# Stick-breaking attention: the causal triangle as a product on TensorE in place of GpSimd's selections

## The chip, the cores and the metric

The kernel runs on one core of a Trainium2 chip. Its time is device microseconds of one execution; a time of a kernel is the median of several executions. The core has five engines, each with a queue of its own that it works through in order: TensorE (PE in the profile, its weight loads PEld), VectorE (DVE), ScalarE (ACT), GpSimd (POOL) and SyncE (SP, which issues DMAs). An instruction waits on semaphores for what other engines have to finish first.

## The reference, cut to what matters

Two transformer blocks run one after the other on 1024 tokens of width 1024. The change lies in the second block's attention, which has 8 heads of 64:

```python
for qb in range(s_len // Q_BLOCK):            # blocks of 128 queries
    z = jnp.einsum('bqhd,bkhd->bhqk', qi, kj) * scale
    causal = s_pos < t_pos
    log_beta = jax.nn.log_sigmoid(z)
    log_rem = jnp.where(causal, jax.nn.log_sigmoid(-z), 0.0)
    suffix = lax.cumsum(log_rem, axis=3, reverse=True) - log_rem
    weights = jnp.where(causal, jnp.exp(log_beta + suffix), 0.0)
    o = jnp.einsum('bhqk,bkhd->bqhd', weights, vj)
```

A weight is the sigmoid of its own score times the product of the sigmoids of the negated scores of all keys between it and the query. Keys at or after the query have a weight of 0, and a factor of 1 in the products.

## The kernel before

All is in fp32. A dense product is made of three products in fp32r, high part by high part, low by high, high by low. The tokens stand in reverse order, so that the suffix of the reference is a running product from the left.

The stage around the change (`ple1_mix2`, from 1625 to 2148 us in the profile) consists of two generators: `dense_in2`, which makes the input projections, the gating, the short convolution and the output projection (`dense_out2`), and `stick_breaking`. `merge_in` takes pieces of the two in an order written out by hand, the string `B_MERGE` (0 for the dense work, 1 for the attention, h for a hook, a piece of work that had been put off). With it the order of the instructions in every engine's queue is fixed; the engines then run each as soon as its semaphores allow.

`stick_breaking` goes through four head pairs p. For each it stacks high and low parts of q and k (`stack`, L1006 to L1024; the low parts get to their place by DMAs from GpSimd's queue), and then goes through 8 query blocks i and the two heads a, 64 blocks in all. Block i has w = 1024 - 128 i columns of keys. Its first 128 columns hold the triangle, the others are all visible. A block consists of these steps:

- L1922: the scores z, two products for each 512 columns, into the PSUM tile ps_s.
- L1925 and L1926 (recorded on L520, in the helper `act`): ScalarE makes rem = sigmoid(-z) and beta = sigmoid(z), both read from PSUM and written to SBUF.
- L1928 and L1929: GpSimd's selections, 128x128 each. The first puts 1 into rem where the key isn't visible, the second 0 into beta.
- L1930: VectorE's scan, a running product along rem.
- L1931: VectorE multiplies beta by the scan, shifted by one column.

Two blocks later (`SB_LAG`) `transposes` turns the weights on TensorE (L1859) in two groups of up to four; ScalarE copies the first group out of PSUM (L1862), VectorE the second (L1864). `product` (L1877) then multiplies by v, and ScalarE copies the result (L1879).

The dense pieces between these are `strip` (L252, with outputs of 128x512) and `token_pair` (L279). Their results leave PSUM on VectorE (L1631 in the projections, L1327 in the output projection, where they are added to x) or in part on ScalarE. Their weights come by DMA, are rounded to a high part by ScalarE (L206), and GpSimd, at times VectorE, makes the low part (L208, 128x1024). GpSimd also has other wide products of 128x1024: the convolution's L1753 and L1758, the gating's L1727, and low parts of the output projection's inputs (y1L, y3L, yb0L, yb1L, yb2L on L701).

At the stage's start `norm_R2` ends with L510 on VectorE, and `dense_in2` loads the gating's constants and lets GpSimd select the lower triangle of one of them, wsT (L1624). Small tiles come from the pool `cst` and stay there; `self.U` gives a tile of 128x1024 from a pool of 41, and it is free again when its last name is gone. `self.masks` (L786) is used in the first block only.

Of the kernel before, what the change touches and what calls it, by code (L numbers as in the profile page):

```python
# [8 lines left out]
F32R = mybir.dt.float32r  # L9
I32 = mybir.dt.int32  # L10
U8 = mybir.dt.uint8
AF = mybir.ActivationFunctionType
ALU = mybir.AluOpType
# [4 lines left out]
P = 128  # L18
# [124 lines left out]
class Kern:  # L143
# [639 lines left out]

    def load_masks(self):
        nc = self.nc
        self.masks = self.cst.tile([P, 8, P], U8, name="masks")  # L786
        t = self.U("mask_f")
        nc.sync.dma_start(out=t, in_=self.aps["c_masks"])
        nc.gpsimd.tensor_copy(out=self.masks, in_=t.rearrange("p (a b) -> p a b", b=P))
# [41 lines left out]
    def block1_mix(self):  # L831
        tc, nc = self.tc, self.nc
        self.scr_hg = self.dram.tile([16, P, 1024], F32, name="scr_hg")
        self.scr_hv = self.dram.tile([4, P, 1024], F32, name="scr_hv")
        self.scr_oda = self.dram.tile([4, P, 1024], F32, name="scr_oda")
        with tc.tile_pool(name="psA", bufs=1, space=PSUM) as psA:
            self.ps_o = self.ps_t = lambda: psA.tile([P, 512], F32, tag="t", name="ps_t", bufs=2)
            self.ps_s = self.ps_n = lambda: psA.tile([P, 1024], F32, tag="s", name="ps_s", bufs=2)
            self.ones = self.cst.tile([P, P], F32, name="ones")
            nc.vector.memset(self.ones, 1.0)  # L840
            self.one_col = self.ones[:, 0:1]
            self.Rc = self.cst.tile([P, 8], F32, name="Rc")

            ps = self.ps_t()[:, 0:P]
            for i in range(16):
                nc.tensor.matmul(ps, self.ones, self.ones, start=True, stop=True)
            ps = None
            self.set_ln()
            st = dict(H=[], L=[])
            xt = []  # L850
            for m in range(KD):
                t = self.U(f"x{m}")
                nc.sync.dma_start(out=t, in_=self.aps["xT"][m])
                xt.append(t)
                if m < 3:
                    self._w_dma(self.upool if m == 2 else None)
            self.load_consts()
            self.raw_qk = {}
            self.first_slots = []
            self.oT = {}  # L860
            self.x = None
            if A_MERGE:
                self.merge_in(A_MERGE, self.dense_mix(st, xt), self.diff_attention(), self.hgrn())
            else:
                self.merge(self.dense_mix(st, xt), self.diff_attention(), self.hgrn())
        self.more_ps = None
        self.dbg("x_mix", self.x)

    def dense_mix(self, st, xt):
# [740 lines left out]
    def dense_in2(self):  # L1610
        nc = self.nc
# [6 lines left out]
        for j in range(2):  # L1618
            for a in range(2):
                nc.sync.dma_start(out=bb[64 * a:64 * a + 64, j], in_=self.aps["sgu_b"][2 * j + a].partition_broadcast(64))  # L1620
        wsT = sgu_c[:, 512:1024].rearrange("p (g t) -> p g t", g=4)
        nc.sync.dma_start(out=wsT, in_=self.aps["sgu_w"])

# [226 lines left out]
    def stick_breaking(self):  # L1850
        nc = self.nc

        def transposes(u, g0):
            gn = min(4, u["n"] - g0)
            if g0 == 0:
                u["T"] = self.U("WT")
            ps = self.ps_t()
            for j in range(gn):
                nc.tensor.transpose(ps[:, j * P:(j + 1) * P], u["W"][:, (g0 + j) * P:(g0 + j + 1) * P], self.ident)  # L1859
            dst = u["T"][:, g0 * P:(g0 + gn) * P]  # L1860
            if g0 == 0:
                nc.scalar.copy(out=dst, in_=ps[:, 0:gn * P])  # L1862
            else:
                nc.vector.tensor_copy(out=dst, in_=ps[:, 0:gn * P])  # L1864
            if g0 + gn == u["n"]:
                u["W"] = None
                turned.append(u)
            return 109 * gn

        def product():  # L1870
            two, turned[:] = turned[:2], turned[2:]
            p, i, n, yb = (two[0][k] for k in ("p", "i", "n", "y"))
            ps = self.ps_o()
            for j in range(n):
                for a in range(2):
                    h = 2 * p + a
                    nc.tensor.matmul(ps[64 * a:64 * a + 64, 0:P], self.vsb[i + j][:, h * 64:(h + 1) * 64], two[a]["T"][:, j * P:(j + 1) * P],  # L1877
                                     start=(j == 0), stop=(j == n - 1))
            nc.scalar.copy(out=yb[:, i * P:(i + 1) * P], in_=ps[:, 0:P])  # L1879
            if i == 7:  # L1880
                self.dbg(f"y_b{p}", [yb])
                if p == 3:
                    self.yT[p] = self.split(yb, f"yb{p}")
                else:
                    nc.sync.dma_start(out=self.scr_y[4 + p], in_=yb)
                self.done.add(f"yb{p}")
            return 268 * n

        def drain(left):
            while len(queue) > left or len(turned) > 1:  # L1890
                if len(turned) > 1:
                    yield product(), 0
                else:
                    u = queue.pop(0)
                    for g0 in range(0, u["n"], 4):
                        yield transposes(u, g0), LAT["sb_t"]

        queue, turned = [], []
        for p in range(4):
            while f"q{p}" not in self.done or f"k{p}" not in self.done:  # L1900
                yield WAIT
            A, B = [], []
            yield from self.stack(self.raw_qk.pop(f"q{p}"), 0.125, "stationary", A)
            yield from drain(2)
            yield from self.stack(self.raw_qk.pop(f"k{p}"), 1.0, "moving", B)
            yield from drain(0)
            yield 0, LAT["sb_head"]
            while "vsb0" not in self.done or "vsb1" not in self.done:
                yield WAIT
            yb = self.U("yb")  # L1910
            for i in range(8):
                n = 8 - i
                w = n * P
                for a in range(2):
                    pd = queue.pop(0) if len(queue) > SB_LAG else None
                    if pd is not None:
                        yield transposes(pd, 0), 0
                    z = self.ps_s()
                    for c0 in range(0, w, 512):
                        cn = min(512, w - c0)  # L1920
                        for part in range(2):
                            nc.tensor.matmul(z[:, c0:c0 + cn], A[a][:, i * P:(i + 1) * P], B[a][part][:, i * P + c0:i * P + c0 + cn],  # L1922
                                             start=(part == 0), stop=(part == 1))
                    beta, rem = self.U("beta"), self.U("rem")
                    self.act(AF.Sigmoid, out=rem[:, 0:w], in_=z[:, 0:w], scale=-1.0)  # L1925
                    self.act(AF.Sigmoid, out=beta[:, 0:w], in_=z[:, 0:w])  # L1926

                    nc.gpsimd.affine_select(out=rem[:, 0:P], in_=rem[:, 0:P], pattern=[[1, P]], compare_op=ALU.is_gt, fill=1.0, base=0, channel_multiplier=-1)  # L1928
                    nc.gpsimd.affine_select(out=beta[:, 0:P], in_=beta[:, 0:P], pattern=[[1, P]], compare_op=ALU.is_gt, fill=0.0, base=0, channel_multiplier=-1)  # L1929
                    nc.vector.tensor_tensor_scan(out=rem[:, 0:w], data0=rem[:, 0:w], data1=self.one_col.to_broadcast([P, w]), initial=1.0, op0=ALU.mult, op1=ALU.min)  # L1930
                    nc.vector.tensor_tensor(out=beta[:, 1:w], in0=beta[:, 1:w], in1=rem[:, 0:w - 1], op=ALU.mult)  # L1931
                    queue.append(dict(p=p, i=i, n=n, W=beta, y=yb))
                    beta = rem = None
                    yield 0.84 * w, 0
                    if len(turned) > 1:
                        yield product(), 0
                    if pd is not None and pd["n"] > 4:
                        yield transposes(pd, 4), 0
                    yield 0, LAT["sb"] + LAT["sb_w"] * w / 1024
        A = B = None  # L1940
        yield 0, LAT["sb"]
        yield from drain(0)
# [277 lines left out]
```

## Time and profile before

| | us |
|---|---|
| median of 3 runs (2973.49 to 2975.86) | 2975.2 |
| the profiled execution | 2975.06 |
| its span, from the first instruction to the last | 2973.3 |
| head pairs of the attention, in the profile | 1753 to 1850, 1850 to 1950, 1950 to 2050, 2050 to 2148 |
| busy: TensorE / VectorE / ScalarE / GpSimd | 2805.6 / 1800.7 / 1150.7 / 976.3 |

A row of the waits names the engine and the instruction that waited, then the one that released it. In the timeline the bracket behind an instruction is the idle time of its engine before it, with the one that released it. PE's rows have modelled ends, and one product's end lies over the next one's start; distances between starts are the better measure. "Granted clock" is the share of TensorE's full clock of 2.4 GHz, of which the chip grants all or half, averaged over a stretch.

### The profile page before, as it was taken

What the parts mean: (1) busy time and instruction counts of PE and PEld (TensorE: products, weight loads), DVE (VectorE), ACT (ScalarE), POOL (GpSimd) and SP (SyncE); (2) the same over time, 40 slices, a digit from 0 to 9 for tenths busy, and PEclk for the clock granted to TensorE, in tenths of its full rate; (3) what the DMA queues carried; (4) which work ended last, traced back from release to release, by engine and by line L of the source; (5) the groups of instructions that cost most, each with busy time, mean ns of one, the idle gap of its engine ahead of it and who ended that gap; (6) DMA issues with size and microseconds to landing.
All of it is one profiled execution on the core that took longest, in us unless ns stands there. A gap on an engine that the chain in (4) does not pass through costs nothing. (4 is left out here: it accounts for less than half of the span.)

```text
span 2973.3 us, 35223 instructions
## 1 busy us (share of the span) xinstructions
PE 2805.6 (94%) x13976; PEld 2320.8 (78%) x13976; DVE 1800.7 (61%) x2090; ACT 1150.7 (39%) x1684; POOL 976.3 (33%) x647
## 2 busy tenths in 40 slices
PE   8999999989899999999999999878899999999999
PEld 7878878877778888777877887656677787888877
DVE  6277676888788777733446465678686444333344
ACT  4245444564543333321234434454364334112131
POOL 2320214665213333221335153343413442223141
PEclk9999999989999999999999999889999999999999
DMA  3321223231312222531113122033133226322112
GB/s 127 83 54 46 79 71 129 102 124 50 107 50 92 85 82 82 200 119 57 57 50 106 43 71 57 29 113 107 36 120 114 105 101 234 127 78 100 39 54 85
DMA packets 73956, 265.23 MB, mean 89 GB/s; under 512 B 8768, under 2 KB 9536, under 8 KB 73792
## 3 DMA queue, kind: packets, MB, share of 16 engines
q1 hardware_dynamic: 49216, 174.90, 16.4%
q10 hardware_dynamic: 20736, 75.51, 7.7%
q0 software_dynamic: 3840, 12.59, 2.0%
q8 instruction: 110, 1.80, 0.3%
q14 instruction: 54, 0.44, 0.0%
HBM read 187.46 MB, written 61.87 MB: 84 GB/s over the span
## 5 line engine op out<-in xcount | busy, mean ns | idle before, releaser
L208 POOL TENSOR_TENSOR WL<-raw,WH 128x1024 fp32r<-128x1024 f32 x120 | 307.1, 2560 | 992.0 <-ACT WH L206 852.7
L1327 DVE TENSOR_TENSOR xr<-xr,psd 128x512 f32<-128x512 f32 x296 | 202.3, 686 | 393.4 <-PE psd L252 391.0
L206 ACT ACTIVATE WH<-raw 128x1024 fp32r<-128x1024 f32 x144 | 151.9, 1056 | 410.6 <-PE psd L252 276.2
L458 PE MATMUL ps_f<-xT,WH 128*128 128x512 f32 x816 | 269.5, 392 | 7.6 <-ACT u L2007 4.9
L458 PE MATMUL psd<-x,WH 128*128 128x512 f32 x800 | 260.8, 392 | 3.8 <-DVE fr L2004 2.6
L252 PE MATMUL psd<-xH,WH 128*128 128x512 f32 x568 | 234.3, 413 | 3.2 <-DVE cv L1652 1.6
L252 PE MATMUL psd<-xL,WH 128*128 128x512 f32 x568 | 224.8, 396 | 0.0
L252 PE MATMUL psd<-xH,WL 128*128 128x512 f32 x568 | 224.4, 395 | 0.0
L458 PEld LDWEIGHTS ps_f<-xT,WH 128*128 128x128 f32 x816 | 153.3, 188 | 45.5 <-ACT u L2007 9.5
L458 PEld LDWEIGHTS psd<-x,WH 128*128 128x128 f32 x800 | 150.8, 189 | 37.8 <-issue 3.9
L458 PE MATMUL ps_f<-xT,WL 128*128 128x512 f32 x408 | 159.1, 390 | 1.6 <-DVE WL L443 1.5
L458 PE MATMUL psd<-x,WL 128*128 128x512 f32 x400 | 156.2, 391 | 0.0
L279 PE MATMUL psd<-WH,xH 128*128 128x256 f32 x448 | 130.0, 290 | 11.2 <-DVE hgst L978 8.8
L1930 DVE TENSOR_TENSOR_SCAN rem<-rem,ones 128x1024 f32<-128x1024 f32 (+7 forms) x64 | 91.6, 1431 | 77.8 <-POOL rem L1928 77.6
L252 PEld LDWEIGHTS psd<-xH,WH 128*128 128x128 f32 x568 | 108.9, 192 | 26.8 <-issue 4.8
L279 PE MATMUL psd<-WL,xH 128*128 128x256 f32 x448 | 128.1, 286 | 1.3 <-POOL WL L208 1.3
L279 PE MATMUL psd<-WH,xL 128*128 128x256 f32 x448 | 127.9, 285 | 0.0
L252 PEld LDWEIGHTS psd<-xL,WH 128*128 128x128 f32 x568 | 108.4, 191 | 24.1
L252 PEld LDWEIGHTS psd<-xH,WL 128*128 128x128 f32 x568 | 108.8, 192 | 21.9 <-issue 1.7
L443 DVE TENSOR_TENSOR WL<-S,WH 128x512 fp32r<-128x512 f32 x136 | 99.3, 743 | 43.7 <-ACT WH L441 43.5
L1102 DVE TENSOR_REDUCE nm<-ps_s 128x1 f32<-128x1024 f32 x64 | 77.6, 1219 | 49.2 <-PE ps_s L1101 49.1
L417 POOL TENSOR_TENSOR S<-raw_b 128x512 f32<-128x512 f32 x30 | 43.9, 1463 | 192.7 <-DMA raw_b<-w_gate 78.8
(809 smaller groups left out, 7595.2 us busy)
## 6 DMA issues: line engine op xcount, KB each, us to landing
raw<-w_in ACTq DMA_DIRECT2D x54, 512.0 KB
scr_f<-fr SPq DMA_DIRECT2D x54, 512.0 KB
fl<-scr_f SPq DMA_DIRECT2D x54, 512.0 KB
raw<-w_ff ACTq DMA_DIRECT2D x32, 512.0 KB
raw<-w_down ACTq DMA_DIRECT2D x22, 512.0 KB
raw_a<-w_ff SPq DMA_DIRECT2D x18, 512.0 KB
scr_hg<-hgst SPq DMA_DIRECT2D x16, 512.0 KB
hg<-scr_hg SPq DMA_DIRECT2D x16, 512.0 KB
```

Source lines behind the costliest of these rows:

```text
L206: nc.scalar.activation(out=self.WH[:, s], in_=raw, func=AF.Copy)
L208: eng.tensor_tensor(out=self.WL[:, s], in0=raw, in1=self.WH[:, s].bitcast(F32), op=ALU.subtract)
L252: nc.tensor.matmul(ps, a, b[:, hs], start=(i == 0), stop=(i == n - 1))
L279: nc.tensor.matmul(ps, a[:, ts], b, start=(i == 0), stop=(i == 23))
L417: diff = lambda out, x, y, op=ALU.subtract: (nc.vector if q["nsum"] < q["head"] + 3 else nc.gpsimd).tensor_tensor(out=out, in0=x, in1=y, o ...
L443: eng.tensor_tensor(out=WL, in0=src, in1=WH.bitcast(F32), op=ALU.subtract)
L458: self.nc.tensor.matmul(ps, x[:, js], y, start=(fresh and j == 0 and e == 0), stop=(j == 3 and e == 2), skip_group_check=True)
L1102: nc.vector.tensor_reduce(out=nm[:, m:m + 1], in_=sc, axis=AX.X, op=ALU.max, negate=True)
L1327: self.nc.vector.tensor_tensor(out=self.x[m][:, hs], in0=self.x[m][:, hs], in1=ps, op=ALU.add)
L1930: nc.vector.tensor_tensor_scan(out=rem[:, 0:w], data0=rem[:, 0:w], data1=self.one_col.to_broadcast([P, w]), initial=1.0, op0=ALU.mult, op1 ...
```

## The change

A constant tile `never` of 128x128 holds -2^100 where the key isn't visible and 0 elsewhere; a second one holds the identity. They are made at the start of `dense_in2`: VectorE clears a tile, GpSimd selects in it once, and ScalarE writes it and the identity as fp32r into the place of `self.masks`, which is given up after the first block. In each of the 64 blocks TensorE adds the product of the identity with `never` to the first 128 columns of the scores, after the first of their two products. The sigmoids then come out as 1 and 0 there, and both selections by GpSimd are dropped. `B_MERGE` and all else stay.

```diff
--- before.py
+++ after.py
@@ -783,7 +783,7 @@
 
     def load_masks(self):
         nc = self.nc
-        self.masks = self.cst.tile([P, 8, P], U8, name="masks")
+        self.masks = self.cst.tile([P, 8, P], U8, tag="masks", name="masks")
         t = self.U("mask_f")
         nc.sync.dma_start(out=t, in_=self.aps["c_masks"])
         nc.gpsimd.tensor_copy(out=self.masks, in_=t.rearrange("p (a b) -> p a b", b=P))
@@ -864,6 +864,7 @@
             else:
                 self.merge(self.dense_mix(st, xt), self.diff_attention(), self.hgrn())
         self.more_ps = None
+        self.masks = None
         self.dbg("x_mix", self.x)
 
     def dense_mix(self, st, xt):
@@ -1618,6 +1619,16 @@
         for j in range(2):
             for a in range(2):
                 nc.sync.dma_start(out=bb[64 * a:64 * a + 64, j], in_=self.aps["sgu_b"][2 * j + a].partition_broadcast(64))
+
+
+        t = self.U("never_f")[:, 0:P]
+        nc.vector.memset(t, 0.0)
+        nc.gpsimd.affine_select(out=t, in_=t, pattern=[[1, P]], compare_op=ALU.is_gt, fill=-2.0 ** 100, base=0, channel_multiplier=-1)
+        c = self.cst.tile([P, 2 * P], F32R, tag="masks", name="never")
+        self.never, self.ident_r = c[:, 0:P], c[:, P:2 * P]
+        nc.scalar.activation(out=self.never, in_=t, func=AF.Copy)
+        nc.scalar.activation(out=self.ident_r, in_=self.ident, func=AF.Copy)
+        t = None
         wsT = sgu_c[:, 512:1024].rearrange("p (g t) -> p g t", g=4)
         nc.sync.dma_start(out=wsT, in_=self.aps["sgu_w"])
 
@@ -1920,13 +1931,12 @@
                         cn = min(512, w - c0)
                         for part in range(2):
                             nc.tensor.matmul(z[:, c0:c0 + cn], A[a][:, i * P:(i + 1) * P], B[a][part][:, i * P + c0:i * P + c0 + cn],
-                                             start=(part == 0), stop=(part == 1))
+                                             start=(part == 0), stop=(part == 1), skip_group_check=True)
+                            if c0 + part == 0:
+                                nc.tensor.matmul(z[:, 0:P], self.ident_r, self.never, start=False, stop=False, skip_group_check=True)
                     beta, rem = self.U("beta"), self.U("rem")
                     self.act(AF.Sigmoid, out=rem[:, 0:w], in_=z[:, 0:w], scale=-1.0)
                     self.act(AF.Sigmoid, out=beta[:, 0:w], in_=z[:, 0:w])
-
-                    nc.gpsimd.affine_select(out=rem[:, 0:P], in_=rem[:, 0:P], pattern=[[1, P]], compare_op=ALU.is_gt, fill=1.0, base=0, channel_multiplier=-1)
-                    nc.gpsimd.affine_select(out=beta[:, 0:P], in_=beta[:, 0:P], pattern=[[1, P]], compare_op=ALU.is_gt, fill=0.0, base=0, channel_multiplier=-1)
                     nc.vector.tensor_tensor_scan(out=rem[:, 0:w], data0=rem[:, 0:w], data1=self.one_col.to_broadcast([P, w]), initial=1.0, op0=ALU.mult, op1=ALU.min)
                     nc.vector.tensor_tensor(out=beta[:, 1:w], in0=beta[:, 1:w], in1=rem[:, 0:w - 1], op=ALU.mult)
                     queue.append(dict(p=p, i=i, n=n, W=beta, y=yb))
```


## Rows read from the trace of the kernel before

**Rows 1.** the page's first part: busy time, share of the span, instructions
```profile
PE 2805.6 (94%) x13976; PEld 2320.8 (78%) x13976; DVE 1800.7 (61%) x2090; ACT 1150.7 (39%) x1684; POOL 976.3 (33%) x647
```

**Rows 2.** stretch, its us, busy us (x count) of PE, PEld, DVE, ACT, POOL; clock; DMA
```profile
1753.00:1850.00 97.00, 93.75 (x577) 75.50 (x576) 66.38 (x71) 46.97 (x76) 40.22 (x44) 1.00 0.21 58
1850.00:1950.00 100.00, 86.62 (x469) 68.90 (x469) 64.92 (x68) 45.16 (x73) 38.02 (x38) 0.90 0.11 34
1950.00:2050.00 100.00, 79.61 (x439) 61.58 (x440) 77.11 (x84) 55.91 (x89) 40.54 (x45) 0.88 0.35 107
2050.00:2148.00 98.00, 79.92 (x462) 61.48 (x462) 68.46 (x71) 40.19 (x72) 42.07 (x46) 0.93 0.24 74
```

**Rows 3.** waits of PE, 1753 to 2148: us in total, times, longest
```profile
PE ps_t L1877 <- DVE WT L1864: 9.7, 7, 3.6
PE ps_t L1859 <- DVE WT L1864: 7.7, 3, 4.4
PE psd L252 <- DVE y0L L701: 7.5, 1, 7.5
PE psd L252 <- DVE xr L1327: 5.0, 2, 2.8
```

**Rows 4.** all waits, 1750 to 2150
```profile
POOL rem L1928 <- ACT rem L520: 161.2, 51, 16.9
DVE rem L1930 <- POOL rem L1928: 77.6, 41, 8.2
```

**Rows 5.** timeline, one block: start, us, engine, line, operation, [idle before <-releaser]
```profile
2089.26 0.92 ACT L520 ACTIVATE rem<-ps_s 128x896 f32<-128x896 f32 x1 [0.91 <-PE ps_s L1922]
2090.26 0.30 POOL L1928 TENSOR_SCALAR_AFFINE_SELECT rem<-rem 128x128 f32<-128x128 f32 x1 [1.89 <-ACT rem L520]
2090.59 2.02 DVE L1930 TENSOR_TENSOR_SCAN rem<-rem,ones 128x896 f32<-128x896 f32 x1 [2.98 <-POOL rem L1928]
```

**Rows 6.** timeline of PE, last score products
```profile
2138.87 0.30 PE L1922 MATMUL ps_s<-stk,stk 128*128 128x128 f32 x1
2139.01 0.28 PE L1922 MATMUL ps_s<-stkl,stk 128*128 128x128 f32 x1
2139.12 0.31 PE L1859 MATMUL ps_t<-ident,beta 128*128 128x128 f32 x1
```

**Rows 7.** timeline of PE, first and last of 13 idle stretches
```profile
1780.94 0.44 PE L1859 MATMUL ps_t<-ident,beta 128*128 128x128 f32 x2 [0.46 <-DVE WT L1864]
...
2144.70 0.79 PE L252 MATMUL psd<-yb2H,WH 128*128 128x512 f32 x1 [2.39 <-ACT yb2H L700]
```

**Rows 8.** timelines of DVE, GpSimd (POOL) and PE, 1856 to 1880
```profile
1856.06 3.40 DVE L1931 TENSOR_TENSOR beta<-beta,rem 128x1023 f32<-128x1023 f32 x1
...
1866.13 2.35 DVE L1930 TENSOR_TENSOR_SCAN rem<-rem,ones 128x1024 f32<-128x1024 f32 x1 [2.76 <-POOL rem L1928]
...
1856.00 2.38 POOL L1753 TENSOR_TENSOR p_h<-p_c,p_h 128x1024 f32<-128x1024 f32 x1
1863.45 2.40 POOL L1758 TENSOR_TENSOR p_b<-p_b,p_c 128x1024 f32<-128x1024 f32 x1 [5.07 <-DVE p_c L1757]
...
1879.17 1.11 PE L1859 MATMUL ps_t<-ident,beta 128*128 128x128 f32 x4 [4.45 <-DVE WT L1864]
```

**Rows 9.** timelines of DVE and GpSimd, around 1976
```profile
1976.71 3.80 DVE L1930 TENSOR_TENSOR_SCAN rem<-rem,ones 128x896 f32<-128x896 f32 x1
1976.25 2.38 POOL L701 TENSOR_TENSOR y1L<-yld,y1H 128x1024 fp32r<-128x1024 f32 x1 [1.14 <-ACT y1H L700]
```

**Rows 10.** timelines of DVE, ScalarE (ACT), GpSimd and PE, 1641 to 1651
```profile
1642.00 0.69 DVE L510 SCALAR_TENSOR_TENSOR R<-rs_u,R 128x512 f32<-128x512 f32 x1
1641.15 1.99 ACT L206 ACTIVATE WH<-raw 128x1024 fp32r<-128x1024 f32 x2
1642.27 5.04 POOL L208 TENSOR_TENSOR WL<-raw,WH 128x1024 fp32r<-128x1024 f32 x2 [8.86 <-ACT WH L206]
1650.46 0.28 PE L279 MATMUL psd<-WH,xH 128*128 128x256 f32 x1
```

## Prediction

> **What bounds the kernel now.** I read the page first: TensorE (PE) is busy 94% of the span and every other engine 61% or less [rows 1]. So PE sets the time, except where it stands idle. The change lies in the stick-breaking stage, so the second view is the table by stretches of that stage, one row for each head pair. There are 55 us in which PE is idle (395.0 long, 339.9 busy), and they are uneven: 3 us of the first 97, then 13, 20 and 18. In the last three the granted clock falls to 0.88 to 0.93: a part of each ran at 1.2 in place of 2.4 GHz [rows 2]. So the first pair is bound by PE, and in the other three PE waits for the chain around it.
>
> Third, the waits. PE's longest are for VectorE (DVE): for the copy of the turned weights out of PSUM (L1864, 9.7 and 7.7 us), for y0L (7.5) and for the additions into x (5.0) [rows 3]. Fourth, what DVE itself waits for: GpSimd's first selection, 77.6 us in 41 times. That looks like the prize, but the row above it says that GpSimd was meanwhile waiting 161.2 us for ScalarE's first sigmoid [rows 4]. Most of DVE's wait is thus ScalarE, and behind it PE, being in no hurry. It will be there after the change too, under ScalarE's name. What the selection itself costs is read from one block: the sigmoid ends at 2089.26 + 0.92 = 2090.18, the selection starts at 2090.26, takes 0.30, and the scan starts at 2090.59 [rows 5]. From sigmoid to scan is 0.41 us. A direct hand-over would keep the 0.08 that GpSimd needed to see the sigmoid, so 0.33 us goes. The second selection lies under the scan, which is 2.02 us long there, and the multiplication needs the scan anyway: I cost its removal at nothing. If the scan were not there to cover it, it would save another 0.3.
>
> **Part 1, the products.** 64 products of 128 columns are added on PE, one a block, each with its weight load. No row before has this product, so I bound it. The nearest are the 128-column products of the last score blocks: starts 0.14 apart (2138.87 to 2139.01), then 0.11 (2139.01 to 2139.12) [rows 6]. Above I take 0.14, 64 x 0.14 = 9.0 us. Below, nothing: the 55 us of idle could hold them all. I take 0.11 each, since the part before it is up to 512 columns long and lets its load run ahead, as the load of the second product there could: 7.0 us in all.
> The Trainium skill ("TensorE: Matmul & The Clock Gate", Part 1) gives 55.6 ns between 128-column matmuls at full clock; by that the 64 would cost an estimated 3.6 us. The same page (Part 2, on LDWEIGHTS) has the load of 128 columns take about 107 ns, whatever the product. The rows side with the load.
> Not all 64 are on the path. The six of blocks 0 to 2 of the second pair lie in the knot below and are counted there; the first eight of the third pair lie ahead of PE idle whose end DVE sets (y0L at 1984.88 among it), which covers them. Were that cover gone they would cost 0.9. That leaves 50 x 0.11 = +5.5 us.
>
> **Part 2, the direct gain.** I went through PE's idle stretches from 1753 to 2148 and followed each one back by the timelines of DVE, ScalarE and GpSimd. In 13 of them a scan that started at its selection's end stands in the chain: the first is 0.46 us before 1780.94, the last 2.39 before 2144.70, which is the end of the stage [rows 7]. Each loses 0.33: -4.3 us. The bounds are zero (another wait steps in) and 64 x 0.33 = 21 us, which would need every block on the path; the count decides for the low end.
>
> **Part 3, the knot.** One place loses more. GpSimd's queue there holds selections and wide products (128x1024, some 2.4 us), and DVE and GpSimd exclude each other: the multiplication of 1856.06 takes 3.40 us, because GpSimd's product started at 1856.00 and ran 2.38. That product had stood behind both selections. Then the scan of 1866.13 waits 2.76 for its selection, which stood behind another product (1863.45, 2.40). The backlog ends with 4.45 us of idle PE before 1879.17, released by DVE's copy [rows 8]. Walked again without selections: the first product, nothing before it in the queue, runs ahead of the scan, and the multiplication loses its 2.3. DVE gains 1.9 of that, since it then waits some 0.4 for PE's next strip. The next scan starts at once: 2.76 more. But the product of 1863.45, released by the step ahead of that scan, now falls between scan and multiplication and takes 2.4 back. -1.9 - 2.8 + 2.4 = -2.2 us at the copy, the six added products included, since PE has the idle to hold them. Bounds: -4.7, if that product waits for both, and 0, if it comes before the scan too.
>
> **Part 4, where no more goes.** In the third pair the long waits are not the selections'. The scan of 1976.71 takes 3.80 us because GpSimd's y1L began at 1976.25, before it, for 2.38 [rows 9], and y0L stands behind it in DVE's queue. y1L stays. I give nothing here; a flip in the order of two such instructions is worth up to 2.4 us, either way.
>
> **Part 5, the constant.** At the stage's start the new selection stands in GpSimd's queue ahead of the one on wsT, and waits for a memset that DVE can only do behind L510 (1642.00 + 0.69). ScalarE's two copies wait for that selection. Behind them are queued two weight splits: ScalarE's (1641.15, 1.99) and GpSimd's (1642.27, 5.04 for two) [rows 10]. By the rows: memset to 1642.9, selection of 0.3 to 1643.2, the copies to 1643.8, the splits' high parts to 1645.8; on GpSimd wsT's selection to 1644.9, and the low parts to 1649.8. PE first needs them at 1650.46, so 0.6 us of cover is left and this costs nothing. If the cover is gone it costs what exceeds it; I put 0.2 (bounds 0 and 2).
>
> **The sum.** +5.5 - 4.3 - 2.2 + 0.2 = -0.8 us. The profiled execution took 2975.06 us (span 2973.3 and 1.8 around it), the median of the runs is 2975.2: so 2974.3 us.
>
> **The rivals.**
> *The backlog goes altogether (faster).* DVE's 77.6 us of waiting gone, it runs ahead, and PE's waits for it close. Those for L1864 and for the additions are 9.7 + 7.7 + 5.0 = 22.4 us [rows 3]; with half of it closed, -11.2, a quarter of the 29 us of clock deficit that the stretches show (0.10 x 100 + 0.12 x 100 + 0.07 x 98) [rows 2] won back with it, -7, and all products, +7.0: 2964. For it: idle and low clock come together, so that a closed gap pays twice. Against it: ScalarE's 161.2 us, and rows 9.
> *PE was the bound (slower).* The idle time doesn't close, because its ends are set by other steps, and PE carries all 64 products: 7.0 to 9.0 us, 2982 to 2984. It decides when less than about 1 us of the 6.5 us of parts 2 and 3 comes. For it: the first pair, with 3 us of idle in 97. Against it: the chains that I followed do pass through the selection.
> *The port goes to GpSimd first.* Without selections in its queue GpSimd reaches its wide products earlier, and where one now starts just before a scan, the scan waits 2.4 us where it waited 0.33. In two places of the chain that is 2 x 2.4 less 2 x 0.33, +4.1: 2978.4. For it: rows 8 and 9 show the exclusion both ways. The Trainium skill ("SBUF — State Buffer", Who interferes with whom) says the same: whichever of the two issues first has the shared port for its whole instruction, and the other blocks fully. That the trace agrees is the 3.40 us of rows 8.
>
> **How the numbers follow.** The forecast 0.47 (its own range 2969 to 2979, from the product at 0 to 0.14 and the gaps of part 2 half or all gained), the backlog 0.28, PE the bound 0.13, the port 0.12. What a measurement of this kernel can tell from no change is 0.2%, 6 us: below 2969.2, above 2981.2. Faster gets 0.25 of the backlog's and 0.05 of the forecast's: 0.30. Slower gets 0.12 of PE's and 0.02 of the port's: 0.14. Within: 0.56. The range leaves out a quarter of the backlog's chance below and PE the bound above: 2962 to 2981.
>
> **What would show it.** In the profile after: the first pair's row longer by 1 to 2 us with PE still at 96 to 97%; DVE's wait for L1928 gone and one of 60 us or more for ScalarE's rem in its place; from sigmoid to scan 0.08 us; the starts around the new product 0.11 apart; the idle before the transposes at 1879 down by about 2 us; the long wait for y0L still there. I am wrong if the y0L wait shrinks by several us or the granted clock of the last three pairs rises (then it is the backlog), or if the products lie 0.2 us or more apart.

## The result: 0.52% faster

| | before | after |
|---|---|---|
| median of 4 runs, us | 2974.34 (2971.51 to 2975.86) | 2956.56 (2955.43 to 2961.58) |
| profiled execution, us | 2975.06 | 2955.43 |
| stage: first score product of the first head pair to the first product with yb2L, us | 390.9 (1756.36 to 2147.23) | 374.9 (1752.90 to 2127.83) |
| PE idle within it, us | 55.1 | 40.35 |

The ratio is 0.9948, with an interval of 0.9936 to 0.9960. That is 17.8 us less, where 0.8 less was forecast; the time lies below the range. It is 7.4 us below even the 2964 of the rival "the backlog goes altogether".

The page's first part after the change, which answers to [rows 1]:

```profile
PE 2800.2 (95%) x14040; PEld 2319.8 (79%) x14040; DVE 1796.2 (61%) x2091; ACT 1151.4 (39%) x1686; POOL 893.9 (30%) x520
```

PE has its 64 products more and is busy 5.4 us less. The stretches tell why: one for each head pair, with the columns of [rows 2]. First come before's last three pairs, cut where the work is the same (its first pair is that of [rows 2]), then the four of after and their sum.

```profile
1850.00:1962.00 112.00, 96.78 (x512) 76.51 (x512) 72.03 (x75) 52.14 (x83) 43.55 (x45) 0.89 0.19 49
1962.00:2060.00 98.00, 79.34 (x448) 61.21 (x446) 79.31 (x85) 52.97 (x85) 40.23 (x44) 0.90 0.31 104
2060.00:2148.00 88.00, 70.02 (x413) 54.24 (x412) 59.14 (x63) 36.16 (x64) 36.84 (x39) 0.92 0.20 66
...
1750.00:1847.00 97.00, 94.91 (x590) 77.10 (x589) 66.83 (x71) 46.58 (x76) 20.27 (x13) 1.00 0.20 57
1847.00:1949.00 102.00, 93.38 (x528) 74.44 (x527) 70.26 (x74) 51.97 (x83) 21.96 (x13) 0.95 0.20 54
1949.00:2046.00 97.00, 79.35 (x467) 62.59 (x466) 82.11 (x87) 53.17 (x85) 22.17 (x12) 0.93 0.32 109
2046.00:2130.00 84.00, 72.01 (x430) 56.96 (x429) 56.22 (x64) 36.29 (x64) 17.98 (x7) 0.90 0.19 65
sum 380.00, PE 339.65 PEld 271.08 DVE 275.42 ACT 188.02 POOL 82.39; mean PE 84.91 PEld 67.77 DVE 68.85 ACT 47.00 POOL 20.60
```

Before's last three pairs were 112, 98 and 88 us long, at a clock of 0.89, 0.90 and 0.92; now they are 102, 97 and 84 at 0.95, 0.93 and 0.90. So two things paid. PE's idle time fell by 14.7 us (395.0 - 339.9 = 55.1 before, 380.0 - 339.65 = 40.35 now). And PE's busy time stayed as it was with 64 products more, because less of it ran at half clock: some 7 us. Only the third pair's idle time hardly changed (18.7 to 17.7 us). The second's fell from 15.2 to 8.6, the fourth's from 18.0 to 12.0.

The waits of the stage answer to [rows 3] and [rows 4]:

```profile
DVE rem L1940 <- ACT rem L520: 64.6, 38, 7.9
...
PE psd L252 <- DVE y0L L701: 7.7, 1, 7.7
...
PE ps_t L1888 <- DVE WT L1875: 5.7, 3, 3.5
PE psd L252 <- DVE xr L1328: 4.1, 2, 2.1
...
PE ps_t L1870 <- DVE WT L1875: 3.5, 3, 2.3
```

VectorE waits 64.6 us for ScalarE where it waited 77.6 for GpSimd. PE's two waits for the copy WT fell from 17.4 to 9.2 us, and y0L's stays.

The knot of [rows 8] looks like this now (GpSimd, VectorE and PE in turn; a timeline's columns are start, us, engine, instruction, and idle time before it):

```profile
1844.98 2.34 POOL L1764 TENSOR_TENSOR p_h<-p_c,p_h 128x1024 f32<-128x1024 f32 x1
1858.04 4.32 POOL L1769 TENSOR_TENSOR p_b<-p_b,p_c 128x1024 f32<-128x1024 f32 x1 [10.71 <-DVE p_c L1768]
...
1857.87 2.28 DVE L1940 TENSOR_TENSOR_SCAN rem<-rem,ones 128x1024 f32<-128x1024 f32 x1
1860.26 3.18 DVE L1941 TENSOR_TENSOR beta<-beta,rem 128x1023 f32<-128x1023 f32 x1
...
1872.55 0.65 PE L1870 MATMUL ps_t<-ident,beta 128*128 128x128 f32 x4 [2.29 <-DVE WT L1875]
```

The convolution's first product p_h, which had stood behind both selections and run beside VectorE's multiplication, is done at 1847.3, three us before the pair's first scan (1850.44). The second, p_b, starts 0.17 us behind the scan, is held up by it and ends at 1858.04 + 4.32 = 1862.36. So it is the multiplication behind the scan that pays, with 3.18 us. PE's idle time falls from 4.45 to 2.29 us.

### The profile page after: what moved, and what is told of

It is laid out like the page before. It is cut to its first block, busy times and chain, and to the rows that moved or that the text cites. A ratio compares the mean times of both kernels' runs of the same rounds, so it can differ in the third digit from the quotient of the medians.

```text
span 2953.7 us, 35084 instructions
## 1 busy us (share of the span) xinstructions
PE 2800.2 (95%) x14040; PEld 2319.8 (79%) x14040; DVE 1796.2 (61%) x2091; ACT 1151.4 (39%) x1686; POOL 893.9 (30%) x520
## 5 line engine op out<-in xcount | busy, mean ns | idle before, releaser
L1940 DVE TENSOR_TENSOR_SCAN rem<-rem,ones 128x1024 f32<-128x1024 f32 (+7 forms) x64 | 92.7, 1449 | 65.1 <-ACT rem L520 64.6
L1103 DVE TENSOR_REDUCE nm<-ps_s 128x1 f32<-128x1024 f32 x64 | 77.6, 1219 | 49.5 <-PE ps_s L1102 49.4
L1105 ACT ACTIVATE E<-ps_s,nm 128x1024 f32<-128x1024 f32 x64 | 71.3, 1115 | 91.7 <-DVE nm L1103 83.5
```

Source lines behind the costliest of these rows:

```text
L1103: nc.vector.tensor_reduce(out=nm[:, m:m + 1], in_=sc, axis=AX.X, op=ALU.max, negate=True)
L1105: nc.scalar.activation(out=e, in_=sc, func=AF.Exp, bias=nm[:, m:m + 1], accum_out=z[:, m:m + 1])
```

## The experiments

**The theory**, formed from the two traces: GpSimd had stood in VectorE's chain twice. (A) Each scan waited for a hop over GpSimd. (C) GpSimd's queue was held until ScalarE's sigmoids were done, so its wide products came late and fell on VectorE's path. By either, VectorE was in arrears, PE waited for it, and with PE's idle time came half clock. **The rivals:** (B) it is the time for which the selections hold the port that GpSimd and VectorE share; or the product itself moved something; or the clock came out luckily.

All runs are built on the kernel after, which differs from before by the products, their two constant tiles and the selections alone. In the table the stage is taken as above and PE's idle time in it likewise; they are of one execution each, so a us or two of theirs is not told from chance, while the experiments' medians are of 5 to 12 runs. Each ratio is to the runs of before on the same chip; a difference between the medians of two rows is not, and by the ratios it comes out up to 2 us otherwise (against after 20.2 us for e2, 15.5 for e3, 10.1 for e4, 16.1 for e6). e6's profiled execution was the fastest of its 12 (2967.2 us).

| run | median us | ratio (interval) | stage us | idle us | busy us |
|---|---|---|---|---|---|
| before | 2974.3 | | 390.9 | 55.1 | 335.8 |
| after | 2956.6 | 0.9948 (0.9936-0.9960) | 374.9 | 40.4 | 334.6 |
| e1 no product | 2954.0 | 0.9941 (0.9928-0.9953) | 370.3 | 42.1 | 328.1 |
| e2 product, both selections | 2976.4 | 1.0016 (1.0008-1.0025) | 394.5 | 50.7 | 343.8 |
| e3 first selection | 2974.0 | 1.0000 (0.9991-1.0009) | 386.9 | 48.7 | 338.2 |
| e4 second selection | 2967.5 | 0.9982 (0.9971-0.9993) | 383.7 | 47.4 | 336.2 |
| e5 both, off the chain | 2960.9 | 0.9960 (0.9947-0.9972) | 377.0 | 41.1 | 336.0 |
| e6 both, one column | 2973.3 | 1.0002 (0.9993-1.0011) | 389.1 | 49.4 | 339.7 |
| e7 queue only | 2962.9 | 0.9969 (0.9958-0.9981) | 381.4 | 42.4 | 339.1 |
| e8 hop over ScalarE | 2963.9 | 0.9971 (0.9960-0.9981) | 380.6 | 43.5 | 337.0 |
| e9 y low parts swapped | 2955.9 | 0.9946 (0.9934-0.9959) | 376.4 | 38.5 | 337.9 |
| e10 y low parts on VectorE | 2955.4 | 0.9940 (0.9928-0.9951) | 373.9 | 38.3 | 335.5 |
| e11 and convolutions | 2955.7 | 0.9941 (0.9929-0.9954) | 373.7 | 35.4 | 338.3 |
| e12 as e11, queue held | 2957.4 | 0.9953 (0.9941-0.9965) | 373.0 | 37.6 | 335.5 |

### What the products cost

e1 takes the line out of the kernel after, so that the causal mask is left out altogether:

```diff
-                            if c0 + part == 0:
-                                nc.tensor.matmul(z[:, 0:P], self.ident_r, self.never, start=False, stop=False, skip_group_check=True)
```

> The changed kernel (2956.6 us) without the 64 products with the constant tile; the selections stay out, so the causal mask on the diagonal blocks is left out altogether. What is read is the price of the 64 products. From the two traces, the stage's time other than TensorE's idle time and its half-clock stretches grew by 6.0 us, 0.094 us for each product: if that is their price, and all of it lies on the path, 2950.6 us. By the forecast's term (5.5 us) 2951.1 us; by the figure of the Trainium skill's page "TensorE: Matmul & The Clock Gate" (55.6 ns, an estimate of 3.6 us) 2953.0 us. If TensorE's idle time takes the products in, nearer to 2955.

e2 puts both selections back and keeps the products:

```diff
+                    nc.gpsimd.affine_select(out=rem[:, 0:P], in_=rem[:, 0:P], pattern=[[1, P]], compare_op=ALU.is_gt, fill=1.0, base=0, channel_multiplier=-1)
+                    nc.gpsimd.affine_select(out=beta[:, 0:P], in_=beta[:, 0:P], pattern=[[1, P]], compare_op=ALU.is_gt, fill=0.0, base=0, channel_multiplier=-1)
```

> The kernel before (2974.3 us) with the products added and both selections kept. If the gain comes from the selections that go and the products only cost, 2978 to 2981 us (plus 3.6 to 6.0). If the gain came from the product itself, by moving TensorE's instructions against each other or by the phase of its clock, near 2957 to 2970 us.

Without the products the median is 2.6 us lower (their intervals overlap) and the stage 4.7 us shorter; with both selections they cost 0.16% (0.08 to 0.25), 4.8 us. So the products are a cost of 3 to 5 us in time and gain nothing. One of them on PE, at full clock, in the first block of the stage:

```profile
1752.90 0.39 PE L1933 MATMUL ps_s<-stk,stk 128*128 128x512 f32 x1
1753.12 0.22 PE L1936 MATMUL ps_s<-never 128*128 128x128 f32 x1
1753.18 0.45 PE L1933 MATMUL ps_s<-stkl,stk 128*128 128x512 f32 x1
1753.46 0.39 PE L1933 MATMUL ps_s<-stk,stk 128*128 128x512 f32 x1
```

The next score product starts only 0.06 us behind it, but the one after that comes 0.28 later instead of 0.23 (before: 1756.36, 1756.59, 1756.82). From the first row to the last it is 0.56 in place of 0.46, some 0.1 for each, and the first pair, with no half clock in it, needed 1.7 us more of PE for its 16.

e1 shows the clock too. It issues exactly before's instructions on PE, and they are 7.7 us less busy (328.1 to 335.8). e2 and after have the same PE instructions as well and differ by 9.2.

### Which selection

e3 puts back the first of the two lines above into the kernel after, e4 the second.

> The changed kernel (2956.6 us) with the first selection (of the 1-minus-sigmoid, on which the scan waits) put back. Theory A, that the selection's place in the chain from sigmoid to scan, with GpSimd's queue ahead of it, keeps VectorE behind: most of the lost 18 us plus 5 us of products comes back, 2970 to 2980 us. Rival B, that it is the time which the selections hold the port that GpSimd and VectorE share: half of it, 2966 to 2969 us, the same as with the second selection alone.

> The changed kernel (2956.6 us) with the second selection (of the sigmoid, awaited by the multiplication behind the scan) put back. The forecast costed it at nothing since the scan covers it: 2956 to 2958 us. If the port or GpSimd's queue, which it holds until ScalarE's second sigmoid is done, is what counted: 2963 to 2970 us.

The first costs 17.4 us by the medians, the second 10.9, and both, in e2, 19.8. Two equal halves, as (B) had it, they are not. The first costs what (A) said, though e3 holds GpSimd's queue as well and can't part (A) from (C). The second, which was to cost nothing, takes over half as much by itself. They don't add up: what each causes is largely the same delay. VectorE's wait for the selection in e4, then GpSimd and VectorE at the knot:

```profile
DVE beta L1942 <- POOL beta L1940: 5.4, 3, 2.5
```

```profile
1861.36 4.31 POOL L1769 TENSOR_TENSOR p_b<-p_b,p_c 128x1024 f32<-128x1024 f32 x1 [5.07 <-DVE p_c L1768]
1865.63 0.54 POOL L1940 TENSOR_SCALAR_AFFINE_SELECT beta<-beta 128x128 f32<-128x128 f32 x2
...
1865.95 1.28 DVE L1942 TENSOR_TENSOR beta<-beta,rem 128x1023 f32<-128x1023 f32 x1 [2.47 <-POOL beta L1940]
```

The selection isn't late by its own 0.3 us. It is queued behind p_b, and the multiplication, whose scan has long ended, waits 2.47 us for it, and 2.48 us at the like place of the third pair.

### Hop, queue or port

e5 lets GpSimd do 128 selections as large as those dropped, from a constant into columns that nobody uses yet. Nothing waits for them, and they wait for no sigmoid.

```diff
+                    nc.gpsimd.affine_select(out=yb[:, 7 * P:8 * P], in_=self.ident, pattern=[[1, P]], compare_op=ALU.is_gt, fill=1.0, base=0, channel_multiplier=-1)
+                    nc.gpsimd.affine_select(out=yb[:, 7 * P:8 * P], in_=self.ident, pattern=[[1, P]], compare_op=ALU.is_gt, fill=1.0, base=0, channel_multiplier=-1)
```

> The changed kernel (2956.6 us) with two selections of 128x128 for each block put back on GpSimd, but from the identity into columns of a tile that are not in use yet: none waits for ScalarE, and nothing waits for them. That leaves their own time and their hold on the port that GpSimd and VectorE share. Theory C (GpSimd's queue, held until ScalarE's sigmoids are done, makes its wide instructions late): 2956 to 2960 us. Theory B (the port time of the selections themselves): 2966 to 2976 us, most of what both selections cost together (19.8 us).

e6 keeps the chain of before and takes the work away, with selections of one column:

```diff
+                    nc.gpsimd.affine_select(out=rem[:, 0:1], in_=rem[:, 0:1], pattern=[[1, 1]], compare_op=ALU.is_gt, fill=1.0, base=0, channel_multiplier=-1)
+                    nc.gpsimd.affine_select(out=beta[:, 0:1], in_=beta[:, 0:1], pattern=[[1, 1]], compare_op=ALU.is_gt, fill=0.0, base=0, channel_multiplier=-1)
```

> The changed kernel (2956.6 us) with both selections put back on one column each (128x1 instead of 128x128): the scan and the multiplication wait for GpSimd, and GpSimd for ScalarE, as before, but the selections hold the port for next to nothing. Theory A (the place in the chain) and theory C (the queue) both: 2970 to 2976 us. Theory B (the port time): 2956 to 2962 us.

e7 holds GpSimd's queue at the sigmoid, and VectorE waits for none of it:

```diff
+                    nc.gpsimd.affine_select(out=yb[:, 7 * P:7 * P + 1], in_=beta[:, 0:1], pattern=[[1, 1]], compare_op=ALU.is_gt, fill=0.0, base=0, channel_multiplier=-1)
+                    nc.gpsimd.affine_select(out=yb[:, 7 * P:7 * P + 1], in_=beta[:, 0:1], pattern=[[1, 1]], compare_op=ALU.is_gt, fill=0.0, base=0, channel_multiplier=-1)
```

> The changed kernel (2956.6 us) with two selections of one column for each block, which read the sigmoid and write a spare tile: GpSimd's queue is held until ScalarE's second sigmoid of the block is done, but VectorE waits for none of it. Theory C (the queue alone): 2965 to 2970 us, about what the second selection alone cost (2967.5 us), or more. Theory A (VectorE's wait for the selection) and theory B (the port time): 2956 to 2959 us.

e8 makes a hop of the same kind without GpSimd:

```diff
                     self.act(AF.Sigmoid, out=rem[:, 0:w], in_=z[:, 0:w], scale=-1.0)
+                    nc.scalar.activation(out=rem[:, 0:1], in_=rem[:, 0:1], func=AF.Copy)
```

> The changed kernel (2956.6 us) with a copy of one column of the 1-minus-sigmoid onto itself by ScalarE between its two sigmoids: the scan waits for this hop as it once did for the selection, but GpSimd has nothing in it. The hop is estimated at 0.2 us. If VectorE's delay in the chain is what costs, whoever makes it, and it counts in about 28 of the 48 blocks of the last three head pairs as the selections' hop did: 5 to 6 us of VectorE, with the clock 2961 to 2966 us. If only GpSimd's queue and port count: 2956 to 2958 us.

e6 is the clearest of them: with 1/128 of the data its time is before's (1.0002). e5 is the counterpart, with all the selections' work (GpSimd is busy 168.1 us in the stage, before 157.6) and 4.3 us lost by the medians (intervals overlap), 2.1 in the stage. So (B) has a small part at most. e7 costs 6.3 us and e8 7.3, by the stage 6.5 and 5.6; their intervals just touch that of after. So hop and queue cost about the same each, and the two together make most of e6's 16.7 (stage 14.1).

The hops as groups (how often, then busy us and mean ns behind the bar): first e8's, then e6's two and VectorE's wait:

```profile
L1939 ACT ACTIVATE rem<-rem 128x1 f32<-128x1 f32 x64 | 13.0, 203 | 2.0
```

```profile
L1941 POOL TENSOR_SCALAR_AFFINE_SELECT beta<-beta 128x1 f32<-128x1 f32 x64 | 47.9, 748 | 15.7 <-ACT beta L520 14.7
...
L1940 POOL TENSOR_SCALAR_AFFINE_SELECT rem<-rem 128x1 f32<-128x1 f32 x64 | 21.2, 332 | 175.7 <-ACT rem L520 171.6 <-DVE hn_R L510 4.0
```

```profile
DVE rem L1942 <- POOL rem L1940: 80.4, 41, 8.3
```

What a hop costs VectorE can be counted in each block: the scan's start, less the later of two ends, that of its sigmoid and that of VectorE's own instruction before. Over the 48 blocks of the last three pairs, 25 scans of before lose 0.39 us on average and two lose 2.76 and 3.66, 16.2 us in all; the other 21 find VectorE still busy and lose nothing. In e6 it is 27 of 0.29 and two of 2.66 and 4.05, in e8 29 of 0.27 (7.8 us). After the change 28 scans find VectorE free and start 0.03 us behind the sigmoid: that much a direct hand-over keeps, so a hop of before cost 0.36 and one of e8 0.24, 7.0 us in all. Beside them stand 7.3 us of time: so most of VectorE's delay in these pairs comes out at the end. It isn't shown that ScalarE's 13.0 us of copies cost nothing of their own.

The two long ones are the queue at work. The first is in [rows 8]; the second was not seen for the forecast (before, GpSimd, ScalarE and VectorE):

```profile
1963.17 2.41 POOL L1758 TENSOR_TENSOR p_b<-p_b,p_c 128x1024 f32<-128x1024 f32 x1 [3.51 <-DVE p_c L1757]
1965.53 2.40 POOL L208 TENSOR_TENSOR WL<-raw,WH 128x1024 fp32r<-128x1024 f32 x1
1967.88 0.30 POOL L1928 TENSOR_SCALAR_AFFINE_SELECT rem<-rem 128x128 f32<-128x128 f32 x1
...
1963.53 1.03 ACT L520 ACTIVATE rem<-ps_s 128x1024 f32<-128x1024 f32 x1 [2.74 <-PE ps_s L1922]
...
1968.21 2.35 DVE L1930 TENSOR_TENSOR_SCAN rem<-rem,ones 128x1024 f32<-128x1024 f32 x1 [4.53 <-POOL rem L1928]
```

The sigmoid is ready at 1964.56 and VectorE idle, but the selection stands behind two wide products. VectorE loses 3.65 us.

In e7 the same happens from the other side (GpSimd, VectorE, PE):

```profile
1853.98 1.31 POOL L1940 TENSOR_SCALAR_AFFINE_SELECT yb<-beta 128x1 f32<-128x1 f32 x1 [6.73 <-ACT beta L520]
...
1855.50 3.40 POOL L1764 TENSOR_TENSOR p_h<-p_c,p_h 128x1024 f32<-128x1024 f32 x1
...
1858.94 0.76 DVE L1766 TENSOR_SCALAR p_c<-p_h,cols 128x1024 f32<-128x1024 f32 x1 [1.70 <-POOL p_h L1764]
...
1877.42 1.11 PE L1870 MATMUL ps_t<-ident,beta 128*128 128x128 f32 x4 [4.67 <-DVE WT L1875]
```

p_h, which in the kernel after had begun at 1844.98, stands behind a sigmoid of 1853.9 with which it has nothing to do. VectorE waits for it, and PE idles 4.67 us where it idled 2.29.

### The wide products, and a try at a better version

e9 swaps the engines of the first four low parts of y (y0L and y2L to GpSimd), e10 gives all four to VectorE, e11 gives it the convolutions' two products too, and e12 is e11 with e7's two lines.

```diff
-            y[j] = self.split(t, f"y{j}", eng=nc.gpsimd if j % 2 else nc.vector)
+            y[j] = self.split(t, f"y{j}", eng=nc.vector if j % 2 else nc.gpsimd)    # e9
+            y[j] = self.split(t, f"y{j}", eng=nc.vector)                            # e10 to e12
...
-            nc.gpsimd.tensor_tensor(out=ah, in0=ac, in1=ah, op=ALU.mult)
+            nc.vector.tensor_tensor(out=ah, in0=ac, in1=ah, op=ALU.mult)            # e11, e12
...
-            nc.gpsimd.tensor_tensor(out=ab, in0=ab, in1=ac, op=ALU.mult)
+            nc.vector.tensor_tensor(out=ab, in0=ab, in1=ac, op=ALU.mult)            # e11, e12
```

> The changed kernel (2956.6 us) with the low parts of the first four loaded strips of y given to the other engine each (the first to GpSimd instead of VectorE, the second to VectorE, and so on). It aims at the largest stall that is left, 7.7 us of TensorE in front of the first of them. If GpSimd is free there, 4 to 7 us less, with the clock: 2949 to 2953 us. If what it waits for is the load behind it, or GpSimd is as late as VectorE: 2955 to 2958 us.

> The changed kernel (2956.6 us) with all four low parts of the first loaded strips of y made by VectorE. In its trace two of them on GpSimd (3.87 and 3.19 us) lengthen a multiplication of VectorE from 1.23 to 2.98 us and a low part from 1.21 to 3.36 us, 3.9 us in all, and save it 2 x 1.21 = 2.4 us. If the port is what makes that stage late: 1 to 4 us less, 2953 to 2956 us. If VectorE's count of instructions is what binds: 1 to 3 us more, 2957 to 2960 us.

> As the run with all four low parts on VectorE, and also the two multiplications of each of the two convolutions moved from GpSimd to VectorE (four instructions; in the changed kernel's trace GpSimd takes 2.40 to 4.32 us for one, and VectorE's scan or multiplication beside it 3.2 to 3.7 us instead of 1.2 to 2.3). If the port binds: a further 1 to 4 us less, 2950 to 2955 us. If VectorE's own work binds: 1.2 us for each, 2958 to 2962 us.

> As the run before it (low parts and convolutions on VectorE), with GpSimd's queue held by two one-column selections for each block that write a spare tile, for which VectorE never waits. With the convolutions on GpSimd that cost 6.3 us (2962.9 against 2956.6 us). If it cost through the convolution's product that stood behind the selections and for which VectorE then waited: 0 to 3 us here. If through the weights' low parts on GpSimd or the port time of the selections: 5 to 7 us here too.

None of e9 to e11 is told from the kernel after (0.9946, 0.9940 and 0.9941 against 0.9948). e11 closes 5 us more of PE's idle time, but its busy time is 3.7 us longer; why is not shown. e12 points to what the queue costs through: 1.7 us against e11 by the medians, where the same two lines cost 6.3 against after, and in the stage -0.7 against 6.5. By the ratios it is 3.6 against 6.2 us, with intervals that overlap, so the time alone doesn't prove it. On the stage's evidence, with p_h, p_b, y1L and y3L off GpSimd, a held queue holds up little that VectorE or PE waits for; the weights' low parts, still on GpSimd, are not the way. e12 at the knot, VectorE and PE:

```profile
1856.59 1.22 DVE L1764 TENSOR_TENSOR p_h<-p_c,p_h 128x1024 f32<-128x1024 f32 x1
...
1875.12 0.66 PE L1870 MATMUL ps_t<-ident,beta 128*128 128x128 f32 x4 [2.84 <-DVE WT L1875]
```

2.84 us of idle PE in place of e7's 4.67.

## Why the prediction was wrong

**What bounds the kernel: right.** In the first pair PE is busy 1.7 us longer for its 16 products; as 1.15 us of idle time went, the pair is only 0.55 us longer, where 1 to 2 had been named. VectorE's wait did go over to ScalarE's name (64.6 of 77.6 us). But I stopped at that remainder. What went, in a chain in arrears, was the prize: before, VectorE has 16.2 us of waiting in the last three pairs of which a direct hand-over keeps less than 1, and PE has lost 14.7 us of idle time.

**Part 1, the products: right in the main.** 0.11 us each was forecast, 7.0 in all, 5.5 of it on the path. The rows give some 0.1, and the path 3 to 5 us. The spacing of 0.06 behind a product is the 55.6 ns of the Trainium skill ("TensorE: Matmul & The Clock Gate", Part 1), which the trace so bears out; the estimate by that alone, 3.6 us, leaves out the 0.05 by which the product behind comes late, and e1 and e2 don't tell the two sums apart.

**Part 2, the direct gain: the step that failed,** in three places. It multiplied 0.33 us by 13 idle stretches of PE. But VectorE carries a delay from block to block until it finds a pause, so that an idle stretch collects the hops of all the blocks since the last one: the count is of blocks in which VectorE was free, 25, and what went of the hop was 0.36 (0.08 had been allowed for the hand-over, which takes 0.03). That is 9.0 us instead of 4.3, and inside the bounds (0 to 21) from which I had decided for the low end. e8 bears the count out. Nor need the stretch behind a hop shrink: the last of the 13, 2.39 us before 2144.70, is 2.39 still, before 2125.31. Next, the second selection at nothing: by itself it costs 10.9 us (e4). The scan covers its 0.3 us, not the 4.31 us of the product that it may be queued behind. Last, the queue: I looked at what GpSimd holds up in one knot, and it does so throughout (e7, 6.3 us). One stretch of the last pair, 2.09 us of idle PE before 2115.17, to which the forecast gave 0.33 at most, is gone. Before, GpSimd and VectorE:

```profile
2111.60 2.37 POOL L208 TENSOR_TENSOR WL<-raw,WH 128x1024 fp32r<-128x1024 f32 x1
...
2111.66 2.99 DVE L1931 TENSOR_TENSOR beta<-beta,rem 128x639 f32<-128x639 f32 x1
```

The same two after:

```profile
2094.07 3.02 POOL L208 TENSOR_TENSOR WL<-raw,WH 128x1024 fp32r<-128x1024 f32 x1 [22.62 <-issue]
...
2094.03 0.83 DVE L1941 TENSOR_TENSOR beta<-beta,rem 128x639 f32<-128x639 f32 x1
```

0.06 us behind GpSimd the multiplication took 2.99 us; 0.04 ahead of it, 0.83. That it fell this way was not foreseen, but neither is it the chance of one execution: it took 2.7 to 3.0 us in all five kernels in which VectorE waits for a selection (before, e2, e3, e4, e6), and 0.82 or 0.83 in the other nine.

**Part 3, the knot: right in size, wrong in extent.** -2.2 us was forecast and 4.45 became 2.29. But two neighbours fell as well, 1.55 us before 1870.55 altogether and 2.75 before 1900.27 to 1.05, and the like knot of the third pair was overlooked. The two engines' order in the knot came as forecast: p_h ahead of the scan, and p_b at the cost of the multiplication.

**Part 4, the third pair: right in the number, by luck.** Its idle time fell by 1.0 us, and the wait for y0L is 7.7 after 7.5. But one of its long waits was a selection's, the 3.65 us above. VectorE won them and lost most of them again to GpSimd's wide products, which it now met. Before, y0L, and after, the scan of the knot, its multiplication and y0L:

```profile
1983.52 1.30 DVE L701 TENSOR_TENSOR y0L<-yld,y0H 128x1024 fp32r<-128x1024 f32 x1
...
1951.47 3.68 DVE L1940 TENSOR_TENSOR_SCAN rem<-rem,ones 128x1024 f32<-128x1024 f32 x1 [0.35 <-ACT rem L520]
1955.24 3.19 DVE L1941 TENSOR_TENSOR beta<-beta,rem 128x1023 f32<-128x1023 f32 x1
...
1968.11 3.36 DVE L701 TENSOR_TENSOR y0L<-yld,y0H 128x1024 fp32r<-128x1024 f32 x1
```

The scan took 3.68 us after 2.35, the multiplication 3.19 after 1.32, and y0L 3.36 after 1.30; only the scan of [rows 9] went the other way, from 3.80 to 2.01. From VectorE's p_k ahead of the knot (1963.00 before, 1950.44 after) to the end of y0L it is 21.8 us before and 21.0 after.

**Part 5, the constant: right.** It cost nothing that shows. A wait of PE ahead of it, before and after:

```profile
1628.50 0.50 PE L1536 MATMUL psd<-xL,WH 128*128 128x512 f32 x1 [1.17 <-DVE xL L1522]
...
1625.05 0.50 PE L1537 MATMUL psd<-xL,WH 128*128 128x512 f32 x1 [1.11 <-DVE xL L1523]
```

From there to the first score product it is 127.86 us before (to 1756.36) and 127.85 after (to 1752.90). The 3.45 us by which the profiled executions differ at that place came ahead of the change; between 1750.3 and 1756.0 the stage begins in the twelve experiments.

**The clock, at nothing in the sum: wrong, the second step that failed.** Half-clock stretches went with the idle time that closed: 7.7 us less of busy PE with the same instructions (before and e1). How much each us of idle is worth stays open: e7 has little idle and 339.1 us busy, e4 more idle and 336.2, so where the stretches fall counts too, and single executions differ.

**The rivals.** "The backlog goes altogether" is nearest to what happened: the granted clock rose in two of the last three pairs, the sign that I had named for it, though the wait for y0L did not shrink and VectorE still waits 64.6 us for ScalarE. Its own terms are close: -11.2 of idle, -7 of clock, +7.0 of products were named, and -14.7, some -7 and +7 were found. What I held against it, ScalarE's 161.2 us, was the wrong argument. GpSimd's waiting for ScalarE wasn't slack; it was the reason why its wide products were late. "The port goes to GpSimd first" was seen with p_b in the first knot (3.18 us) and in the third pair, where VectorE's busy time rose from 79.4 to 81.7 us (from its first score product to the next pair's). But such meetings were there before too, and in all they cost no more than they had: over the stage VectorE's 291 instructions were busy 273.6 us before and 272.5 after. ([rows 8] and [rows 9] show VectorE blocked behind GpSimd alone; the other way round is p_b's 4.32 us behind the scan.) "PE was the bound" needed less than 1 us of the gaps to close.

## What to carry to other kernels

A tiny instruction in an in-order queue costs its place, not its time: ask what the instructions behind it have to wait for, and behind what it stands itself. When a chain runs in arrears, count a saved hop once for each step at which the late engine was free, not once for each stall of the engine that bounds the kernel; and look for what the late engine will meet once it is early. And where stalls and low clock come together, put a price on the clock.

## What the runs showed of the hardware

A selection of one column is not always short. Two of e7's, and the scan of VectorE in the same us:

```profile
1868.18 0.18 POOL L1940 TENSOR_SCALAR_AFFINE_SELECT yb<-beta 128x1 f32<-128x1 f32 x1
1868.43 1.89 POOL L1941 TENSOR_SCALAR_AFFINE_SELECT yb<-beta 128x1 f32<-128x1 f32 x1
...
1868.34 2.01 DVE L1942 TENSOR_TENSOR_SCAN rem<-rem,ones 128x896 f32<-128x896 f32 x1
```

The second starts 0.09 us into the scan and ends at 1870.32, the scan at 1870.35: the selection took 0.18 us where it began ahead of VectorE's scan and 1.89 where the scan was first. That is the rule of the Trainium skill ("SBUF — State Buffer", Who interferes with whom) that the later one blocks for the whole of the earlier one's instruction. The trace agrees, and adds that it holds for one element a partition (1.89 us) as for 1024 (p_b's 4.32).
